# An RMS norm that writes each row twice: loads moved to ScalarE's queue and ahead of each tile's compute, engines in written order, last tile in two halves

## Chip, cores, metric

One core of one Trainium2 chip. The metric is the device time of one execution in microseconds (us). The profile's *span* runs from the first to the last recorded instruction. A run is called fast or slow; a slow run is one that took over 1.5% more than the fastest of the same kernel.

## The reference

```python
B, S, D = 8, 512, 2048                     # x: 8 x 512 x 2048 float32, gamma: 2048
x_rep = np.repeat(x, 2, axis=1)
rms = np.sqrt((x_rep ** 2).mean(axis=-1, keepdims=True) + 1e-6)
return x_rep / rms * gamma                 # 8 x 1024 x 2048 float32
```

The least traffic is one read of x (33.55 MB) and one write of the output (67.11 MB).

## The kernel before

Eight tiles of 128 partitions x 4 rows. A tile buffer holds 8 output rows; the 4 input rows are loaded into its second half and overwritten in place. Three buffers. All loads and stores are issued by SyncE; the framework's scheduler orders the instructions of each engine.

```python
K = 4                                              # rows per partition and tile
rows  = ctx.enter_context(tc.tile_pool(name="rows", bufs=3))
# ... (other pools cut)
def load(i, parts=1):
    y = rows.tile([P, K * R, D], f32, name="y")
    step = K // parts
    for k in range(0, K, step):
        at = K * (R - 1) + k
        nc.sync.dma_start(out=y[:, at : at + step, :], in_=x_t[i, :, k : k + step, :])
    ys.append(y)

load(0, parts=K)
# ... (gamma on ScalarE's queue, broadcast to the partitions; eps)
load(1)
load(2)
for i in range(ntiles):                            # ntiles = 8
    y = ys[i]
    for k in range(K):
        # ... (xk = input row k, y0 and y1 = its two output rows)
        nc.scalar.activation(out=sq[:], in_=xk, func=Act.Square, accum_out=ss[:])
        nc.scalar.activation(out=rms[:], in_=ss[:], func=Act.Sqrt, scale=inv_d, bias=eps_t[:])
        nc.vector.reciprocal(out=rstd[:], in_=rms[:])
        nc.vector.scalar_tensor_tensor(out=y0, in0=xk, scalar=rstd[:], in1=gamma_b[:],
                                       op0=Alu.mult, op1=Alu.mult)
        if k == K - 1:
            nc.vector.tensor_copy(out=y1, in_=y0)
        else:
            nc.scalar.copy(out=y1, in_=y0)
    nc.sync.dma_start(out=out_t[i], in_=y.rearrange("p j d -> p (j d)"))
    if i >= 1 and i + 2 < ntiles:
        load(i + 2)
```

## Time and profile before

| | before |
|---|---|
| time, median of 3 runs | 240.31 us (239.82 to 240.62) |
| profiled run | 240.86 us, span 239.1 us |
| DVE (VectorE) / ACT (ScalarE) busy | 37% / 49% of the span |
| DMA | 98.3% of 16 engines' span, 421 GB/s |

In the profile's lines SPq and ACTq are the sequencers of SyncE and ScalarE, which issue DMAs; q1 is SyncE's DMA queue and q10 ScalarE's; L71 is line 71 of the kernel; `y<-in_x_dram` is a load of x into a tile and `out_dram<-y` a store. A DMA *lands* when its completion is recorded.

From the page of the kernel before: a line of the queue section (packets, MB, share of 16 engines), the chain that ended last by engine, the squares' line of the instruction groups (busy us, mean ns, then idle before it and its releaser), and two lines of the DMA issues (count, KB each where one size, median us from issue to landing).

```profile
q1 hardware_dynamic: 2736, 100.66, 98.3%
...
DMA 68%; ACT 13%; DVE 8%; SPq 1%; issue 1%
...
L71 ACT ACTIVATE sq<-y 128x2048 f32<-128x2048 f32 x32 | 59.7, 1865 | 92.5 <-DMA y<-in_x_dram 92.5
...
y<-in_x_dram SPq DMA_DIRECT2D x7, 4096.0 KB, 38.8
...
out_dram<-y SPq DMA_DIRECT2D x8, 32.0
```

The first line is the one that decides. One queue carries everything and keeps the 16 engines busy for 98.3% of the span. The chain shows 21% of compute, and the squares waited 92.5 us for loads, but neither is time to be won: while one tile is loaded or computed, another tile's transfer fills the engines. The windows view shows it (columns: stretch in us, its length, busy us and instruction count of each engine, TensorE clock, DMA share, GB/s):

```profile
60.00:110.00 50.00, 11.11 (x9) 14.24 (x15) 0.00 (x0) 1.00 0.98 422
110.00:160.00 50.00, 22.21 (x18) 28.49 (x30) 0.00 (x0) 1.00 1.01 435
160.00:210.00 50.00, 16.37 (x15) 24.80 (x27) 0.00 (x0) 1.00 1.02 438
210.00:215.00 5.00, 4.93 (x4) 3.69 (x4) 0.00 (x0) 1.00 0.97 419
215.00:220.00 5.00, 0.91 (x1) 0.00 (x0) 0.00 (x0) 1.00 1.01 433
```

Engine work swings between 11 and 28 us per 50, the DMA rate hardly moves (422 to 438 GB/s). (This view books a packet's bytes at its start, so short windows swing by a few per cent to either side.)

The packet records of the trace give the floor. A packet here is one contiguous run of one partition: 64 KB in a store, 32 KB in a load, 8 KB in the first tile's loads. Their median times are 2.418, 1.213 and 0.309 us, so each engine moves about 27 GB/s in either direction (26.5 with the 8 KB packets). Each of the 16 engines has 64, 56 and 32 of them: 232.6 us of pure packet time.

### The profile page before, as it was taken

The numbers are of one execution on the slowest core, as the hardware profiler recorded it, in microseconds if no ns is written. First come the engines' busy times: TensorE is split into PE (matmuls) and PEld (weight loads), VectorE is DVE, ScalarE is ACT, GpSimd is POOL, SyncE is SP. The second block draws the span as 40 slices with busy tenths as digits, with TensorE's granted clock in tenths as the row PEclk, the third lists the DMA queues.
The fourth block names the chain that finished last, engine by engine and source line by source line (L and its number), as shares of the span: only waits on it lengthen the run. The fifth ranks groups of instructions, "written<-read, shape, count | busy, mean of one in ns | idle before, by whom it ended". The sixth has DMA issues, their size and how long they took to land.

```text
span 239.1 us, 293 instructions
## 1 busy us (share of the span) xinstructions
DVE 88.8 (37%) x73; ACT 116.3 (49%) x122; POOL 2.5 (1%) x5
## 2 busy tenths in 40 slices
DVE  0449759590000085400863016820168202591000
ACT  2998999950000299104990059800598006970000
POOL 4000000000000000000000000000000000000000
DMA  7999998989899999899898999899989899898984
GB/s 262 426 454 439 439 439 351 526 351 526 351 428 439 493 395 451 384 411 510 362 515 351 439 439 506 373 422 433 493 384 471 362 461 461 384 482 384 493 384 175
DMA packets 2741, 100.69 MB, mean 421 GB/s; under 512 B 306, under 2 KB 306, under 8 KB 306
## 3 DMA queue, kind: packets, MB, share of 16 engines
q1 hardware_dynamic: 2736, 100.66, 98.3%
q14 instruction: 3, 0.02, 0.0%
q10 hardware_dynamic: 2, 0.01, 0.0%
HBM read 33.56 MB, written 67.11 MB: 421 GB/s over the span
## 4 chain that ended last, share of the span: by engine, by line
DMA 68%; ACT 13%; DVE 8%; SPq 1%; issue 1%
DMA y<-in_x_dram 41%; DMA out_dram<-y 27%; ACT sq L71 7%; DVE y L76 6%; ACT y L83 5%; DVE y L81 2%; SPq L52 1%; ACT rms L73 1%; DVE rstd L75 0%; SPq L84 0%
## 5 line engine op out<-in xcount | busy, mean ns | idle before, releaser
L71 ACT ACTIVATE sq<-y 128x2048 f32<-128x2048 f32 x32 | 59.7, 1865 | 92.5 <-DMA y<-in_x_dram 92.5
L76 DVE SCALAR_TENSOR_TENSOR y<-y,rstd,gamma_b 128x2048 f32<-128x2048 f32 x32 | 75.3, 2352 | 1.2
L75 DVE RECIPROCAL rstd<-rms 128x1 f32<-128x1 f32 x32 | 5.1, 159 | 124.8 <-ACT rms L73 124.8
L83 ACT COPY y<-y 128x2048 f32<-128x2048 f32 x24 | 44.7, 1890 | 3.2 <-DVE y L76 3.2
L81 DVE COPY y<-y 128x2048 f32<-128x2048 f32 x8 | 9.8, 1226 | 0.3
L73 ACT ACTIVATE rms<-ss,eps_t 128x1 f32<-128x1 f32 x32 | 9.4, 293 | 0.7
L71 ACT ACTIVATION_READ_ACCUMULATOR sq<-y 128x1 f32 x32 | 6.0, 186 | 0.0
L58 POOL PARTITION_BROADCAST gamma_b<-gamma_b x1 | 2.3, 2293 | 2.1 <-DMA gamma_b<-in_gamma_dram 2.1
L71 ACT ACT_TABLE_LOAD x1 | 1.3, 1283 | 1.3 <-PEq L101 1.3
L73 ACT ACT_TABLE_LOAD x1 | 1.3, 1283 | 0.0
L60 DVE MEMSET eps_t<- 128x1 f32 x1 | 0.1, 59 | 0.8 <-PEq L101 0.8
L101 POOL MEMSET const-bfloat16-1.0<- 128x1 bf16 x1 | 0.1, 101 | 0.0
L101 POOL MEMSET const-uint8-127<- 128x1 uint8 x1 | 0.1, 101 | 0.0
L101 POOL MEMSET const-float32-0.0<- 128x1 f32 x1 | 0.1, 98 | 0.2 <-issue 0.2
L101 POOL MEMSET const-float32-1.0<- 128x1 f32 x1 | 0.1, 99 | 0.0
## 6 DMA issues: line engine op xcount, KB each, us to landing
y<-in_x_dram SPq DMA_DIRECT2D x7, 4096.0 KB, 38.8
y<-in_x_dram SPq DMA_DIRECT2D x4, 1024.0 KB, 8.0
out_dram<-y SPq DMA_DIRECT2D x8, 32.0
gamma_b<-in_gamma_dram ACTq DMA_DIRECT2D x1, 8.0 KB
```

The source lines that it names most:

```text
L52: nc.sync.dma_start(out=y[:, at : at + step, :], in_=x_t[i, :, k : k + step, :])
L58: nc.gpsimd.partition_broadcast(out_ap=gamma_b[:], in_ap=gamma_b[0:1, :])
L60: nc.vector.memset(eps_t, eps)
L71: nc.scalar.activation(out=sq[:], in_=xk, func=Act.Square, accum_out=ss[:])
L73: nc.scalar.activation(out=rms[:], in_=ss[:], func=Act.Sqrt, scale=inv_d, bias=eps_t[:])
L75: nc.vector.reciprocal(out=rstd[:], in_=rms[:])
L76: nc.vector.scalar_tensor_tensor(out=y0, in0=xk, scalar=rstd[:], in1=gamma_b[:], op0=Alu.mult, op1=Alu.mult,)
L81: nc.vector.tensor_copy(out=y1, in_=y0)
L83: nc.scalar.copy(out=y1, in_=y0)
L101: nc = _bacc.Bacc("TRN2", target_bir_lowering=False, num_devices=1)
```

## The change

The intent: a load shall no longer stand behind a store in one queue; loads run ahead; the last tile is stored in two parts so that its end is short. Loads go to ScalarE's queue, stores to SyncE's. ScalarE issues the load of tile i+1 before the compute of tile i. A manual schedule replaces the scheduler, and the next row's square is written ahead of this row's copy. The last load and the last store are cut in halves, and the store of the sixth tile is issued in 32 KB runs.

```diff
-    def load(i, parts=1):
+    def load(i, eng, parts=1):
...
-            nc.sync.dma_start(out=y[:, at : at + step, :], in_=x_t[i, :, k : k + step, :])
+            eng.dma_start(out=y[:, at : at + step, :], in_=x_t[i, :, k : k + step, :])
...
+    def store(i, k0, k1):
+        run = 32768 if i == ntiles - 3 else 65536
+        nc.sync.dma_start(
+            out=out_t[i, :, R * k0 * D : R * k1 * D],
+            in_=ys[i][:, R * k0 : R * k1, :].rearrange("p j d -> p (j d)"),
+            max_dma_last_dim=run,
+        )
...                                  (square, scale and repeat: the old operations as functions)
+    def compute(i, k0, k1):
+        rms = square(i, k0)
+        for k in range(k0, k1):
+            scale(i, k, rms)
+            if k + 1 < k1:
+                rms = square(i, k + 1)
+                repeat(i, k, nc.scalar.copy)
+            else:
+                repeat(i, k, nc.vector.tensor_copy)
+    ctx.enter_context(tc.manual_schedule())
-    load(0, parts=K)
+    load(0, nc.scalar, parts=K)
...                                  (gamma to SyncE's queue; loads 1 and 2 on ScalarE's)
     for i in range(ntiles):
...                                  (old loop body cut)
-        nc.sync.dma_start(out=out_t[i], in_=y.rearrange("p j d -> p (j d)"))
-        if i >= 1 and i + 2 < ntiles:
-            load(i + 2)
+        if i >= 2 and i + 1 < ntiles:
+            load(i + 1, nc.scalar, parts=2 if i + 2 == ntiles else 1)
+        parts = 2 if i == ntiles - 1 else 1
+        for k in range(0, K, K // parts):
+            compute(i, k, k + K // parts)
+            store(i, k, k + K // parts)
```

More of the change, by code (lines that the diff above doesn't have):

```diff
@@ L51, in load, with square, scale, repeat @@
             at = K * (R - 1) + k
-            nc.sync.dma_start(out=y[:, at : at + step, :], in_=x_t[i, :, k : k + step, :])
+            eng.dma_start(out=y[:, at : at + step, :], in_=x_t[i, :, k : k + step, :])
         ys.append(y)
-    load(0, parts=K)
+    def store(i, k0, k1):
[5 more added lines that the diff above has]
+        )
+    def square(i, k):
+        sq = junk.tile([P, D], f32, name="sq")
+        ss = small.tile([P, 1], f32, name="ss")
+        nc.scalar.activation(
+            out=sq[:], in_=ys[i][:, K * (R - 1) + k, :], func=Act.Square, accum_out=ss[:]
+        )
+        rms = small.tile([P, 1], f32, name="rms")
+        nc.scalar.activation(out=rms[:], in_=ss[:], func=Act.Sqrt, scale=inv_d, bias=eps_t[:])
+        return rms
+    def scale(i, k, rms):
+        rstd = small.tile([P, 1], f32, name="rstd")
+        nc.vector.reciprocal(out=rstd[:], in_=rms[:])
+        nc.vector.scalar_tensor_tensor(
+            out=ys[i][:, R * k, :], in0=ys[i][:, K * (R - 1) + k, :], scalar=rstd[:], in1=gamma_b[:],
+            op0=Alu.mult, op1=Alu.mult,
+        )
+    def repeat(i, k, copy):
+        copy(out=ys[i][:, R * k + 1, :], in_=ys[i][:, R * k, :])
+    def compute(i, k0, k1):
[9 more added lines that the diff above has]
+    load(0, nc.scalar, parts=K)
     gamma_b = singles.tile([P, D], f32, name="gamma_b")
-    nc.scalar.dma_start(out=gamma_b[0:1, :], in_=gamma.partition_broadcast(1))
+    nc.sync.dma_start(out=gamma_b[0:1, :], in_=gamma.partition_broadcast(1))
     nc.gpsimd.partition_broadcast(out_ap=gamma_b[:], in_ap=gamma_b[0:1, :])
@@ L60 @@
     nc.vector.memset(eps_t, eps)
-    load(1)
-    load(2)
+    load(1, nc.scalar)
+    load(2, nc.scalar)
     for i in range(ntiles):
-        y = ys[i]
-        for k in range(K):
-            xk = y[:, K * (R - 1) + k, :]
-            y0, y1 = y[:, R * k, :], y[:, R * k + 1, :]
-            sq = junk.tile([P, D], f32, name="sq")
-            ss = small.tile([P, 1], f32, name="ss")
-            nc.scalar.activation(out=sq[:], in_=xk, func=Act.Square, accum_out=ss[:])
-            rms = small.tile([P, 1], f32, name="rms")
-            nc.scalar.activation(out=rms[:], in_=ss[:], func=Act.Sqrt, scale=inv_d, bias=eps_t[:])
-            rstd = small.tile([P, 1], f32, name="rstd")
-            nc.vector.reciprocal(out=rstd[:], in_=rms[:])
-            nc.vector.scalar_tensor_tensor(
-                out=y0, in0=xk, scalar=rstd[:], in1=gamma_b[:],
-                op0=Alu.mult, op1=Alu.mult,
-            )
-            if k == K - 1:
-                nc.vector.tensor_copy(out=y1, in_=y0)
-            else:
-                nc.scalar.copy(out=y1, in_=y0)
-        nc.sync.dma_start(out=out_t[i], in_=y.rearrange("p j d -> p (j d)"))
-        if i >= 1 and i + 2 < ntiles:
-            load(i + 2)
+        if i >= 2 and i + 1 < ntiles:
[4 more added lines that the diff above has]
+            store(i, k, k + K // parts)
 _INS = ['x', 'gamma']
```

## The prediction

> **What bounds the kernel now.** The DMA engines do. The page's queue section puts 98.3% of the 16 engines' span on one queue, which carries all loads and stores; DVE is busy 37%, ACT 49%. The trace's packet records give the floor: a 64 KB store packet takes 2.418 us (median), a 32 KB load packet 1.213, an 8 KB one 0.309: 27.1, 27.0 and 26.5 GB/s per engine, so direction and size hardly matter. Per engine, 64 store packets (154.8 us), 56 large load packets (67.9) and 32 small ones (9.9) make 232.6 us (estimate) of the 239.1 us span. The rest is about 1.6 us before the first packet, some 4 us of slow packets, ramp and engines that finish late (the last by 1.4 us), and 1.0 us after the last landing. The Trainium skill, "DMA: Bandwidth & Descriptors", section "Where 436 GB/s comes from", gives a ceiling of 435 GB/s; 16 x 27.1 = 433 here agrees. There is no gap in mid-kernel: the windows view shows 413 to 459 GB/s from 5 us to 230 us. The chain of waits (DMA 68%, ACT 13%, DVE 8%) looks as if compute were on the path; it is not, because another tile's transfer fills the engines meanwhile.
>
> **What the change does.**
> - Loads and stores get a queue each. Same bytes, same 16 engines. The skill, same page, section "Issuing engines are not separate DMA queues", says that this only saves sequencer time; that is 0.33 to 0.66 us per DMA in the trace, hidden already. Worth 0.
> - A load no longer stands behind a store, but shares the engines with it packet by packet. This reorders bytes in a full pipe. Loads should land about 30 us after issue (now 38.8), stores about 35 us (now 32.0).
> - The load of tile i+1 stands on ACT before tile i's compute, so ACT waits there for store i-2. A tile has 28.9 us of DMA and some 17 us of compute, so this wait is slack.
> - Written order: about 17.2 us of compute per tile instead of 16.5. Off the path.
> - More packets: one store of 32 KB runs, the last load in 16 KB runs, the last store in 32 KB runs. A split costs about 8 ns (2 x 1.213 - 2.418): estimate 0.8 us in all.
> - Last tile in halves: ready at about 205 us instead of 215.9, but its store starts only when store 6 leaves the engines (about 216 us both times). Worth 0 to 0.5. A read beside a write may hide some of the 1.5 us (mean per engine) that slow load packets cost, or make more of them: plus or minus 1.5.
>
> So almost nothing of it lies on the critical path.
>
> **Predicted time:** 239.0 us, range 236.8 to 241.8. Faster by over 2% (under 235.5): 0.04; that would need nearly all of the loss at both ends gone. Within 2%: 0.90. Slower: 0.06.
>
> **What would show it.**
> - Right: 98 to 99% DMA share, on two queues (about 33% and 66%); packet medians unchanged, or up to double if an engine works at a packet of each queue at once; first packet at 1.6 us; the last landing 1 us before the end; about 430 GB/s throughout.
> - ACT's idle time before the squares moves into the queue's wait for stores, with no dip in DMA.
> - Wrong: windows below 400 GB/s in mid-kernel (ACT's wait starves the pipe, or mixed directions slow the memory), or above 440.
>
> **What would make it wrong.** Mixed reads and writes running at another rate than either alone; loads starved beside 64 KB store packets, so that the last tile is late and the end runs dry; engines drifting apart with two queues, which lengthens the tail.

## The result, and the profile after

| | before | after |
|---|---|---|
| time, median of 4 runs | 240.28 us | 240.86 us (240.71 to 240.96) |
| profiled run: time, span | 240.86, 239.1 us | 240.80, 239.0 us |
| ratio of fast runs | | 1.0025 (95%: 1.0007 to 1.0043) |

A ratio is the mean time of one kernel's fast runs over that of the other's of the same rounds, so it is not quite the ratio of the medians.

The same lines of the page after (the loads now have a queue, a line and a count of their own):

```profile
q1 hardware_dynamic: 1426, 67.12, 65.0%
q10 hardware_dynamic: 1728, 33.56, 33.3%
...
DMA 71%; ACT 10%; DVE 8%; ACTq 1%; issue 0%; SPq 0%
...
L67 ACT ACTIVATE sq<-y 128x2048 f32<-128x2048 f32 x32 | 59.9, 1872 | 90.3 <-DMA y<-in_x_dram 74.4
...
y<-in_x_dram ACTq DMA_DIRECT2D x6, 4096.0 KB, 32.6
...
out_dram<-y SPq DMA_DIRECT2D x6, 37.5
```

and its windows:

```profile
60.00:110.00 50.00, 18.14 (x15) 22.48 (x24) 0.00 (x0) 1.00 1.00 434
110.00:160.00 50.00, 22.40 (x18) 28.71 (x30) 0.00 (x0) 1.00 1.03 445
160.00:210.00 50.00, 17.36 (x14) 22.68 (x24) 0.00 (x0) 1.00 1.00 429
210.00:215.00 5.00, 4.51 (x4) 4.44 (x6) 0.00 (x0) 1.00 1.03 446
215.00:220.00 5.00, 1.66 (x2) 0.00 (x0) 0.00 (x0) 1.00 0.74 321
```

65.0% and 33.3% on two queues are the old 98.3%. Loads land 32.6 us after issue instead of 38.8, stores 37.5 instead of 32.0: bytes were reordered in a full pipe. (The 321 GB/s of the last window is the booking at packet starts; by the packet records the engines' idle time in the whole middle of the run is 0.1 us each.)

For the rest of this document the packet records of each trace are put into one sum: *floor* is all packets at their median time for their size, per engine; *slow* is what packets took beyond that; *idle* is time in which engines had no packet, in the first 5 us, in the middle, and in the last 6 us before the last packet's end; *rest* runs from there to the span's end. The parts add up to 0.4 to 1.3 us more than the span, because records of successive packets overlap slightly.

| profile | floor | slow | idle, start | idle, middle | idle, end | rest | span |
|---|---|---|---|---|---|---|---|
| before | 232.6 | 2.2 | 1.9 | 0.3 | 1.1 | 1.4 | 239.1 |
| after | 232.8 | 2.0 | 1.9 | 0.1 | 1.5 | 1.3 | 239.0 |

Nothing moved. So there were two questions for the chip. Why was a gain of 0.5% forecast that was not there? And are the parts of the change really worth nothing each, or do they cancel?

### The profile page after: what moved, and what is told of

Same layout as the page of the kernel before. It is cut to its first block, busy times and chain, and to the rows that moved or that the text cites. A ratio compares the mean times of both kernels' runs of the same rounds, so it can differ in the third digit from the quotient of the medians.

```text
span 239.0 us, 295 instructions
## 1 busy us (share of the span) xinstructions
DVE 90.8 (38%) x74; ACT 115.8 (48%) x121; POOL 2.5 (1%) x5
## 3 DMA queue, kind: packets, MB, share of 16 engines
q10 hardware_dynamic: 1728, 33.56, 33.3%
## 4 chain that ended last, share of the span: by engine, by line
DMA 71%; ACT 10%; DVE 8%; ACTq 1%; issue 0%; SPq 0%
DMA y<-in_x_dram 38%; DMA out_dram<-y 33%; DVE y L77 6%; ACT sq L67 6%; ACT y L83 3%; DVE y L83 2%; ACTq L52 1%; ACT rms L71 1%; DVE rstd L76 0%; SPq L58 0%
## 5 line engine op out<-in xcount | busy, mean ns | idle before, releaser
L67 ACT ACTIVATE sq<-y 128x2048 f32<-128x2048 f32 x32 | 59.9, 1872 | 90.3 <-DMA y<-in_x_dram 74.4
L83 ACT COPY y<-y 128x2048 f32<-128x2048 f32 x23 | 43.4, 1888 | 3.6 <-DVE y L77 3.6
L83 DVE COPY y<-y 128x2048 f32<-128x2048 f32 x9 | 11.0, 1226 | 0.3
## 6 DMA issues: line engine op xcount, KB each, us to landing
y<-in_x_dram ACTq DMA_DIRECT2D x6, 4096.0 KB, 32.6
out_dram<-y SPq DMA_DIRECT2D x6, 37.5
```

The source lines that it names most:

```text
L67: nc.scalar.activation(out=sq[:], in_=ys[i][:, K * (R - 1) + k, :], func=Act.Square, accum_out=ss[:])
L83: copy(out=ys[i][:, R * k + 1, :], in_=ys[i][:, R * k, :])
```

## The experiments

Letters used in the expectations: theory A says that the pipe of DMA engines is full in both kernels and that my 239.0 us was a span put against a time; B that a real gain was eaten by the second queue; C that the split last tile costs. All results were correct unless said. 15 runs on five chips, each beside runs of the kernel before.

### The change again, twice

No edit.

> The changed kernel once more, beside the kernel before on this chip. Theory A (the pipe of 16 DMA engines is full in both; my 239.0 us was the profile's span, and the measured time lies some 1.8 us above the span whatever the kernel): time minus span 1.8 us in every run; ratio to before 0.998 to 1.004, and if the first +0.25% was real the span is longer by the same 0.5 us. Theory B (the gain I forecast, -0.5%, was there, and the second queue costs it again, +1.8 us): the same ratio here, but the two parts run beside it lie apart from each other by over 1 us.

Measured: median 240.82 us over 6 runs, of which two were slow (248.49 and 247.54); ratio of fast runs 1.0003 (0.9972 to 1.0033). Time minus span was 1.7 to 1.8 us in each.

> The changed kernel a third time. Ratio of fast runs to before 0.997 to 1.004 again, time minus span 1.7 to 1.8 us. If the slow runs (247 to 249 us, two of six before) belong to the changed kernel, one or more of six again and none of the kernel before; if to that chip or moment, none.

Measured: median 240.86 us over 6 runs, one slow (244.82); ratio 1.0036 (1.0009 to 1.0062). The profiles of these two are of a 239.73 us and a 242.70 us run of one and the same kernel, and the sum tells where the 3 us lie: idle at the end 0.6 against 3.4, everything else equal within 0.2. In the second, one engine finished 3.5 us after most of the others. So the 0.1 to 0.9 us of the three ratios is smaller than this scatter of the last engines. Whether the change makes it larger is not settled: two of three intervals exclude 1.

In every run that lists both, 240 to 269 us long, the time is 1.73 to 1.84 us above the span. That is theory A's first half.

### The second queue taken away again

```diff
-            load(i + 1, nc.scalar, parts=2 if i + 2 == ntiles else 1)
+            load(i + 1, nc.sync, parts=2 if i + 2 == ntiles else 1)
```
(likewise the first three loads; gamma back to ScalarE's queue)

> The changed kernel with its loads on SyncE's queue again (gamma on ScalarE's, as before); order, halves and packet sizes as changed. A: within 0.5 us of before and of the changed kernel. B (the second queue costs what the rest gains): 1.0 us or more faster than the changed kernel, so about 239.0 us. C (the ends, that is the split last tile and its smaller packets, cost the 0.25%): as the changed kernel, 240.8.

Measured: 240.25 us, ratio 0.9983 (0.9959 to 1.0008), no slow run in 6. B is out as stated: its 239.0 us, a ratio of about 0.995, lies outside the interval. Beside the changed kernel on the same chip the fast runs lie 0.2 us (means) to 0.4 us (medians) lower; that the second queue costs some tenths of a us is not excluded. This version does not beat the kernel before clear of noise either.

### The last tile whole

```diff
-        run = 32768 if i == ntiles - 3 else 65536
+        run = 65536
-            load(i + 1, nc.scalar, parts=2 if i + 2 == ntiles else 1)
+            load(i + 1, nc.scalar, parts=1)
-        parts = 2 if i == ntiles - 1 else 1
+        parts = 1
```

> The changed kernel with the last tile whole: one last load, one last store, all stores in 64 KB packets. A: within 0.5 us of the changed kernel, and the DMA engines never run dry at the end, because the last tile is ready (about 210 us) before store 6 leaves them (about 216). C: back to 240.2, faster than the changed kernel by 0.3 to 0.8 us. If loads starve beside 64 KB stores, the last load lands late and the time grows by several us.

Measured: 242.20 us, ratio 1.0070 (1.0031 to 1.0109), one slow run (250.51). Neither A nor C: the halves, with the smaller packets that go with them, were not worth nothing, and they do not cost. All five fast runs (241.16 us and more) lie above all four of the changed kernel on this chip (240.95 and less). Windows of its profile (a 244.24 us run, the slowest of the five, so its dry stretch is no measure of the usual loss):

```profile
210.00:215.00 5.00, 3.23 (x3) 4.97 (x6) 0.00 (x0) 1.00 0.97 419
215.00:220.00 5.00, 3.46 (x4) 3.46 (x4) 0.00 (x0) 1.00 0.06 26
220.00:225.00 5.00, 0.54 (x1) 0.00 (x0) 0.00 (x0) 1.00 0.98 419
```

The engines ran dry at 216.8 us for 4.7 us: the store of the seventh tile was through, and the last tile was still being computed; its store was issued at 220.6. In the changed kernel the second half is no earlier ready than 216.8 either, but the first half's store (issued 196.9) covers it. I had estimated 205 us for the whole.

### The queues exchanged and nothing else

On the kernel before:

```diff
-            nc.sync.dma_start(out=y[:, at : at + step, :], in_=x_t[i, :, k : k + step, :])
+            nc.scalar.dma_start(out=y[:, at : at + step, :], in_=x_t[i, :, k : k + step, :])
-    nc.scalar.dma_start(out=gamma_b[0:1, :], in_=gamma.partition_broadcast(1))
+    nc.sync.dma_start(out=gamma_b[0:1, :], in_=gamma.partition_broadcast(1))
```

> The kernel before with only the queues exchanged: loads on ScalarE's queue, stores on SyncE's, order and last tile as before. A: within 0.5 us of before, unless the last load, which now shares with a 64 KB store, lands so late that the last tile misses the end of store 6: then slower by the time that the engines run dry (some us). B: 1.0 us or more slower than before with no dry stretch.

Measured: 264.12 us, ratio 1.0973 (1.0947 to 1.1000). My first term, "a queue each, worth 0", is 24 us wrong as soon as it stands alone. The engines run dry four times, at 110.3, 145.8, 181.1 and 216.6 us, for 5.0 to 5.2 us each. Windows around the second:

```profile
140.00:145.00 5.00, 0.00 (x0) 0.00 (x0) 0.00 (x0) 1.00 0.73 315
145.00:150.00 5.00, 1.42 (x3) 3.75 (x4) 0.00 (x0) 1.00 0.01 2
150.00:155.00 5.00, 4.84 (x5) 4.97 (x8) 0.00 (x0) 1.00 0.98 419
```

and what the engines did there, from the timeline (start us, us, engine, line, operation, then the idle time before it and its releaser):

```profile
125.26 2.35 DVE L76 SCALAR_TENSOR_TENSOR y<-y,rstd,gamma_b 128x2048 f32<-128x2048 f32 x1
146.21 1.88 ACT L71 ACTIVATE sq<-y 128x2048 f32<-128x2048 f32 x1 [21.18 <-DMA y<-in_x_dram]
...
148.58 0.16 DVE L75 RECIPROCAL rstd<-rms 128x1 f32<-128x1 f32 x1 [20.96 <-ACT rms L73]
148.66 1.21 DVE L81 COPY y<-y 128x2048 f32<-128x2048 f32 x1
...
149.93 0.33 SPq L84 DMA_DIRECT2D out_dram<-y  x1
```

A tile's last scaling ends at 127.6. Only its last copy is missing, 1.2 us of work. But the copy stands on VectorE behind a reciprocal of the *next* tile, that waits for the next tile's square, and that for the next load, which lands at 146.2. So the finished tile is stored at 149.9, after 21 us of waiting, and by then the engines have nothing left. With the load's issue on ScalarE's queue the scheduler had put VectorE's copy after the reciprocal for the fourth, fifth and sixth tile, and for the seventh a ScalarE copy after the eighth's first square. In the kernel before, the copy follows its scaling at once, and the store waits for no load:

```profile
124.01 2.35 DVE L76 SCALAR_TENSOR_TENSOR y<-y,rstd,gamma_b 128x2048 f32<-128x2048 f32 x1
126.39 1.23 DVE L81 COPY y<-y 128x2048 f32<-128x2048 f32 x1
127.68 0.33 SPq L84 DMA_DIRECT2D out_dram<-y  x1
```

In the order of VectorE's instructions these three copies are the only difference between the two traces. Four stores chained to the next load; four dry stretches.

Two readings were open: the chain (D), or that loads are now issued late, in the middle of a tile (L).

### The late copy alone

On the changed kernel:

```diff
         nc.vector.reciprocal(out=rstd[:], in_=rms[:])
+        while held:
+            held.pop(0)()
...
-                repeat(i, k, nc.vector.tensor_copy)
+                held.append(lambda: (repeat(i, k, nc.vector.tensor_copy), store(i, k0, k1)))
```
(and `store` taken out of the loop; what is left in `held` runs at the end)

> The changed kernel with one thing taken from the order that the queue split got from the scheduler: the last VectorE copy of a tile, and so its store, stands behind the first reciprocal of the next tile, which waits for the next load. Theory D (the store of tile i chained to the landing of load i+1, which itself shares the engines with store i-1, is what makes the split cost 24 us): dry stretches of some us per tile in the DMA engines, time 250 to 266 us. Theory L (the split costs because a load is issued late on ScalarE's queue): loads are as early as in the changed kernel, so 240 to 242 us.

Measured: 258.12 us, ratio 1.0707 (1.0690 to 1.0724). D's range, but look at the wait before believing it. Here a tile's store was issued 4.1 us after ScalarE issued a load (85.54 and 89.64 us, for instance), and that load waits for the store two tiles back to land. So stores run one at a time, with five dry stretches of 1.5 to 1.8 us. The sum has 9.5 us idle in the middle and 10.9 us of slow packets against 2.0 in the changed kernel. A late copy costs 17 us here, through another wait than in the split kernel.

### The late copy on one queue

The same kernel with its loads on SyncE's queue, in program order.

> The run with the late copy (258.1 us) with its loads put on SyncE's queue, in front of the stores and in the same program order; the engines' order is untouched. If the late copy costs 17 us only because two queues share the engines (the next load then lands as late as the store ahead of it drains, so both queues run empty together): with one queue the load of the tile after next is already queued behind and covers the gap, 239.5 to 243 us. If the order on the engines costs it by itself: 254 us or more.

Measured: 258.33 us, ratio 1.0728 (1.0699 to 1.0756). My expectation failed: with one queue the loss is the same. In program order the load stands in front of the late store on SyncE, and waits for the store before to land; the store was issued right after it (85.67 and 86.10 us). Dry stretches of 1.6 to 2.1 us. This pair does not isolate the split kernel's chain; it shows only that a store behind the next tile's start is dear on either number of queues.

### Loads in the middle of a tile

On the changed kernel, VectorE's order untouched:

```diff
                 rms = square(i, k + 1)
+                if k == 1 and late is not None:
+                    late()                       # the load of tile i + 1, for i >= 3
```
(and no load ahead of the compute, except the fourth tile's)

> The changed kernel with each load from the fifth tile on issued in the middle of the tile before it, after its third square, as the scheduler placed it in the split kernel; VectorE's order as changed. L: dry stretches, 255 us or more. D: the load meets an emptier store queue, lands within some 15 us of its issue, and the time stays at 239.5 to 242 us.

Measured: 250.83 us, ratio 1.0432 (1.0365 to 1.0498). Between both expectations: D alone said at most 242, L at least 255. There are 8.4 us idle in the middle, most of it in two stretches, at 159.2 (3.8 us) and at 234.3 (3.3 us), where the last loads, issued at 183.6, took 44.1 us (median of the two) to land. So on this kernel the place of the load matters also. (It is not what costs the split kernel its time: see the run with the chain cut, which leaves the loads where they are.)

### Smaller store packets in the split kernel

```diff
-        nc.sync.dma_start(out=out_t[i], in_=y.rearrange("p j d -> p (j d)"))
+        nc.sync.dma_start(out=out_t[i], in_=y.rearrange("p j d -> p (j d)"), max_dma_last_dim=16384)
```
The instructions of every engine stay in the order of the 264.1 us kernel, chain and all.

> The kernel with only the queues exchanged (264.1 us), same instruction order on every engine, but every store in 16 KB packets in place of 64 KB. Sharing theory (the engines take one packet of each queue in turn, whatever its size, so a 32 KB load packet gets a third of the engines beside 64 KB store packets and two thirds beside 16 KB ones): loads land about 23 us after issue in place of 29, the dry stretches go, and the time is 241.5 to 244.5 us including about 1.7 us for more packets. If engines are shared by bytes, or the order on the engines alone sets the loss: 262 to 268 us.

Measured: 240.80 us (240.80 to 240.91), ratio 0.9992 (0.9977 to 1.0006). One argument takes all 24 us back. The DMA issues of the split kernel:

```profile
y<-in_x_dram ACTq DMA_DIRECT2D x7, 4096.0 KB, 28.8
...
out_dram<-y SPq DMA_DIRECT2D x8, 29.2
```

and with 16 KB store packets:

```profile
out_dram<-y SPq DMA_DIRECT2D x8, 8192.0 KB, 34.9
y<-in_x_dram ACTq DMA_DIRECT2D x7, 4096.0 KB, 19.6
```

The Trainium skill, "DMA: Bandwidth & Descriptors", section "Queues, rings and completion order", says that an engine takes the queues that have work in turn, packet by packet. The traces agree: where both queues had work in the changed kernel (55 to 105 us) the records count 208 store and 224 load packets, and here (85 to 100 us) 143 and 128; put into 16 sequences by their start times, store and load packets alternate nearly one by one. So the share in *bytes* is set by the packet sizes: a 32 KB load gets a third beside 64 KB stores and two thirds beside 16 KB stores. With two thirds the load lands well before the store beside it is through, the chain is released in time, and the chain costs nothing. Four packets for one raise the floor from 232.6 to 234.3 us; the time does not show it (the records overlap 0.9 us more, and the slow packets and idle ends are about 0.9 us less).

### No compute

Squares, scalings and copies left out, half of each buffer set to one on VectorE.

```diff
         ys.append(y)
+        nc.vector.memset(y[:, 0 : K, :], 1.0)
...
-            compute(i, k, k + K // parts)
```

> Wrong on purpose: the changed kernel's loads and stores with all squares, scalings and copies left out (the first half of each tile is set to one on VectorE, so the same bytes are stored). Theory A (both kernels are the engines' packet time, 232.6 us, plus fixed ends): 239.5 to 243 us, so compute costs next to nothing in either kernel; the upper end if the stores, which now start at about 11 us, delay the last load. If compute were on the critical path as the chain of waits shows it (ACT and DVE together 18 to 21%): well under 230 us.

Measured: 241.96 us, ratio 1.0066 (1.0018 to 1.0114), result wrong. Without any of the 116 us of ScalarE and 91 us of VectorE work the kernel is not faster. (VectorE is not quite idle: the fills take 55.1 us, and each store waits for its fill.)

```profile
L54 DVE MEMSET y<- 128x8192 f32 x8 | 55.1, 6885 | 120.3 <-issue 118.7
```

This is the plainest proof that the 21% of compute in the chain of waits was not time to be won. (Two runs took 240.7, two 243.3 us; the profile is of a 243.47 us run and has 4.0 us idle at the end.)

### More work on ScalarE, before and after

One more square per row block, its result thrown away, in each kernel:

```diff
+        extra = junk.tile([P, D], f32, name="sq")
+        nc.scalar.activation(out=extra[:], in_=..., func=Act.Square)
```

> The kernel before with one more square per row block on ScalarE (about 7.5 us more per tile, result thrown away). A: nothing in mid-kernel, where the next store has some 10 us of slack; at the end the last tile, which was ready 1 us before the engines ran dry, is now 6 to 7 us late: 245 to 249 us with one dry stretch at about 217 us.

Measured: 251.96 us, ratio 1.0476 (1.0444 to 1.0508). The stretch at the end is there, but longer than I worked out, and there are two small ones early (1.5 and 2.0 us at 31.6 and 52.5 us):

```profile
215.00:220.00 5.00, 1.73 (x3) 5.00 (x5) 0.00 (x0) 1.00 0.97 419
220.00:225.00 5.00, 1.73 (x3) 4.69 (x5) 0.00 (x0) 1.00 0.00 0
```

ScalarE is busy and the engines stand still for 8.4 us from 221.1: the kernel before has hardly any slack for its last tile.

> The changed kernel with the same addition. A: the first half of the last tile covers the second, so the end does not run dry; 240.5 to 243 us. If the order with loads ahead has less slack in mid-kernel than the kernel before (there a store is issued about 8 us before the store ahead of it drains, estimate from its trace): dry stretches in mid-kernel and 244 us or more.

Measured: four runs, 242.63, 247.25, 248.11 and 248.86 us. Only the first counts as fast. The profile fell on a slow run; it has no dry stretch of the last tile (2.6 us idle in the middle, of which 1.9 at 51 us), but 6.7 us of slow packets. That the changed kernel bears more ScalarE work at its end is seen in this one profile of a slow run; that it is faster with it is shown by one run only, and whether the other three are this kernel's usual time is open.

### A tiny store at the start

On the kernel before, because in every trace so far the load packets just ahead of the first store took longer:

```diff
+    first = singles.tile([P, 16], f32, name="first")
+    nc.vector.memset(first[:], 0.0)
+    nc.scalar.dma_start(out=out_t[0, :, 0:16], in_=first[:])
     load(0, parts=K)
```

> The kernel before with one tiny store (64 bytes per partition, overwritten later by the first tile's store) issued on ScalarE's queue at the start. In every trace so far the last load packets before the first store took about 1.0 to 1.2 us longer per engine. If the first write of the run causes that stall, it moves to the start and may overlap the ramp there: 239.3 to 240.3 us, and no slow packets at about 30 us. If it comes from something else: the slow packets stay at 30 us and the time is 240 to 241.2 us.

Measured: 240.58 us, ratio 1.0006 (0.9975 to 1.0038), and the slow packets are still at 25 to 33 us (1.2 us per engine). It is not the first write as such. Its profile (a 242.08 us run) also shows a dry stretch of 1.1 us at 217 us: the narrow end of the kernel before was missed in this run.

### The split kernel with its chain cut

The split kernel's order on every engine, written out by hand (compared instruction by instruction with the 264.1 us kernel: the same), with four moves (given here in words; the edit itself rewrites the loop):

```diff
   VectorE, fourth, fifth and sixth tile
     scalar_tensor_tensor   last row of this tile
+    tensor_copy            last row of this tile, then its store
     reciprocal             first row of the next tile
-    tensor_copy            last row of this tile, then its store
   ScalarE, seventh tile
+    copy                   third row of this tile, then its store
     square                 first row of the eighth tile
-    copy                   third row of this tile, then its store
```

> The split-only kernel with its order written out by hand (the same instructions in the same order on every engine as the 264.1 us run), but for four moves: the last VectorE copy of the fourth, fifth and sixth tile goes in front of the next tile's first reciprocal, and the last ScalarE copy of the seventh in front of the eighth's first square. If the chain (store of a tile behind the landing of the next load) is the cost: the four dry stretches of 5.2 us go, 240 to 244 us. If the late place of the loads on ScalarE's queue is: the stretches stay in part, 248 to 256 us. If it is the sharing of the engines by itself: 262 us or more.

Measured: 241.92 and 243.14 us in the fast runs, 246.27 and 253.54 in two slow ones. The profile, of the 243.14 us run, has one dry stretch of 0.7 us instead of four of over 5; idle in the middle fell from 21.3 to 1.2 us. The timeline of it answers to that of the split kernel:

```profile
134.88 2.35 DVE L76 SCALAR_TENSOR_TENSOR y<-y,rstd,gamma_b 128x2048 f32<-128x2048 f32 x1
137.27 1.23 DVE L85 COPY y<-y 128x2048 f32<-128x2048 f32 x1
138.56 0.33 SPq L55 DMA_DIRECT2D out_dram<-y  x1
141.06 1.88 ACT L62 ACTIVATE sq<-y 128x2048 f32<-128x2048 f32 x1 [6.41 <-DMA y<-in_x_dram]
```

The copy comes right after its scaling, and the store is issued *before* the next load lands. The loads are issued at the same places in ScalarE's order as in the split kernel, so their late place does not make the loss: even the two slow runs here lie 10 us and more below every run of the split kernel. What is left above the kernel before, some 2 us by two fast runs, is mostly slow packets (4.6 us), which no run explains.

### The chain on one queue

The hand-written order of the 264.1 us kernel on ScalarE and VectorE, with loads and stores on SyncE's queue.

> The split-only order on ScalarE and VectorE, chain and all, with loads and stores in one queue, each store ahead of the load that comes after it. If the chain costs by itself (the load lands only after the store ahead of it has left, and the next store comes 4 us after that landing): about the same dry stretches, 260 to 268 us. If the second queue is needed for the loss: 240 to 246 us.

Measured: 268.69 us, ratio 1.1180 (1.1166 to 1.1195), dry for 10.5 us at 110.3 and for 5.1 to 5.2 us at 150.8, 186.0 and 221.2.

```profile
151.39 1.88 ACT L62 ACTIVATE sq<-y 128x2048 f32<-128x2048 f32 x1 [21.38 <-DMA y<-in_x_dram]
...
153.75 0.16 DVE L72 RECIPROCAL rstd<-rms 128x1 f32<-128x1 f32 x1 [21.16 <-ACT rms L67]
153.83 1.21 DVE L85 COPY y<-y 128x2048 f32<-128x2048 f32 x1
...
155.10 0.34 SPq L55 DMA_DIRECT2D out_dram<-y  x1
```

The same picture without a second queue: the load lands, 3.7 us later the finished tile is stored. So the order of four instructions costs this without a second queue too; moving the loads led the scheduler to it. The order needs a load that lands late: with 16 KB store packets, where it lands early, the same order cost nothing.

### The sums side by side

| profile | floor | slow | idle, start | idle, middle | idle, end | span |
|---|---|---|---|---|---|---|
| split only | 232.6 | 5.3 | 2.0 | 21.3 | 0.1 | 262.2 |
| split, chain cut | 232.6 | 4.6 | 1.9 | 1.2 | 0.1 | 241.4 |
| split, 16 KB stores | 234.3 | 1.8 | 2.0 | 0.1 | 0.7 | 239.0 |
| chain, one queue | 232.6 | 4.6 | 1.9 | 26.6 | 0.1 | 266.8 |
| change, late copy | 232.8 | 10.9 | 2.0 | 9.5 | 0.3 | 256.3 |
| change, mid-tile load | 232.8 | 4.8 | 1.9 | 8.4 | 0.1 | 248.8 |
| change, last tile whole | 232.6 | 2.0 | 2.0 | 4.8 | 0.1 | 242.5 |
| change, one queue | 232.8 | 1.9 | 1.9 | 0.1 | 1.2 | 238.6 |

The floor is 232.6 to 234.3 us in all; nearly everything that was gained or lost here is in the columns "idle, middle" and "slow". In the late-copy run the slow packets follow each dry stretch within 15 us, but the run with the chain cut has 4.6 us of them with one short stretch. What makes them is not shown.

## Why the prediction was right or wrong

**The step that failed is the last one, "Predicted time: 239.0 us".** The sum before it (1.6 us to the first packet, 232.6 of packets, about 4 of slow packets, ramp and late engines, 1.0 at the end) is a sum of the *span*. It gave about 239 us, and the span after the change was 239.0 us. But I wrote it down as the time, whose value before was 240.3, and so forecast a gain of 0.5% directly under the sentence that almost nothing of the change lies on the critical path. The missing term is the 1.7 to 1.8 us by which the time exceeds the span in every run. With it the same sum says 240.8; measured was 240.86. So close a hit is partly luck: two of the forecast's smaller terms, the halves and the extra packets, were wrong (below).

**The bound was right.** The engines' packet time is the floor, directions and queues do not matter to it, and removing all compute did not help (241.96 us). The skill's section "Where 436 GB/s comes from" (the same page) gives 435 GB/s as the ceiling of the fabric; 16 engines at 27.0 to 27.1 make 432 to 434 here. No version beat both kernels; the nearest, the changed kernel on one queue, has a ratio of 0.9983 with 1 inside its interval.

**"Loads and stores get a queue each. Worth 0" was right within some tenths of a us on the finished kernel and wrong for the step.** Alone it costs 24 us, because the order that the scheduler then chose chains four stores to the next tile's load (264.1; with only these four cut, about 242.5). The skill's sentence that a second issuing engine only saves issue time holds for bandwidth: the floor is the same 232.6. It says nothing of what the queue's waits do to the order of an engine that also computes.

**"Written order: off the path" was wrong in the same way.** Its 17.0 us per tile are off the path, as forecast. But the order is what keeps each store in front of the next load; written order together with loads ahead takes 264.1 back to 242.2 (last tile whole). On the changed kernel late loads cost 10 us (250.8) and late copies 17 (258.1), the copies through another wait; these are other losses than the split kernel's. The clean test of that one is the four moves, which left the loads late and removed all but some 2 us of it.

**"Last tile in halves: worth 0 to 0.5" was too small.** Against the whole tile the halves are worth about 1.4 us (medians of fast runs on one chip: 242.0 and 240.6), and they cover a loss that the change itself brings. I had the last tile ready at 205 us; it was 216.8, because its load landed 39.7 us after issue. The halved load goes in 16 KB packets beside stores of 32 KB and then 64 KB, and took 27% of the packet time from 168 to 188 us and 21% from 188 to 208.

**Extra packets: 0.8 us was too much.** The floor rose by 0.2 us. At 8 ns a split, 0.8 us would be 100 splits on each engine; each has 24.

**Signs.** Two queues of 65.0 and 33.3%, medians of 2.418 and 1.213 us, loads at 32.6 us (forecast 30) and stores at 37.5 (35) came as written. ScalarE's wait did move only in part: 15.9 us of its idle time ended by a store, 74.4 still by loads. My alarm of 400 GB/s per window was no good: a window of 321 appeared with no engine idle.

**Open.** The 0.25%: two of three measurements are clear of 1, it is within the scatter at the end, and a cost of the second queue of this size is not excluded. And the slow runs: in kernels that use both queues 9 of 51 runs took 1.5 to 5% more than the fastest of their kernel, in kernels with all large transfers on one queue 0 of 76. They fell on three of the five chips, where the kernel before had none in 34 runs. The only profile of such a run has many slow packets (6.7 us); why, no run shows. Three of the nine are the runs with more ScalarE work, which may be that kernel's usual time.

## What to carry to other kernels

When the DMA engines are full, a change of queues or order cannot gain, but it can lose: look at what each store waits for, and make sure that no instruction a finished tile still needs stands behind one that waits for the next load. Two queues share the engines by packets, so packet size sets who gets the bytes, and can repair an order or ruin it. And before a sum of the profile is called a time, put the profile's span beside the measured time of the same run.

## What the Trainium skill lacked or had wrong

- "DMA: Bandwidth & Descriptors", "Queues, rings and completion order": the turn-taking by packets is there, with a packet of typically 9 to 17 descriptors. That section does not say how many bytes a turn moves. In the records here a turn was one contiguous run of up to 64 KB, 128 runs in a full store, so that the shares in bytes follow the run lengths: loads landed after 28.8 us beside 64 KB stores and 19.6 us beside 16 KB stores.
- The same page, "Issuing engines are not separate DMA queues": right on bandwidth (floor 232.6 and 232.8 us). It lacks that moving the issues to an engine that also computes can change the order that a scheduler gives the engines: from about 240.6 to 264.1 us with only the queues exchanged in the source.
- No page that I found has it: the last load packets before the first large store took 1.0 to 1.3 us longer per engine in most runs, and an early small store did not remove it.
- "Runtime: NRT & Kernel Launch" would be the place for it, and lacks it (the gap that it describes is between two other times): the time lay 1.7 to 1.8 us above the span from the first to the last recorded instruction, in runs of 240 to 269 us alike.
- No page that I found has it: single-core slow runs with both queues in use, 9 of 51 against 0 of 76. (The clock of 1.0 that all of them list says nothing here: TensorE has no work, and the traces hold no clock records.)
